# Attention scores as three products of high and low parts, and a bank test for TensorE work, in a two-layer float32 backbone on one core

## The chip, the cores and the metric

The kernel runs on one NeuronCore of a Trainium2 chip. The metric is the device time of one execution in microseconds (us), taken as the median of several runs. Five engines work side by side, each through its own list of instructions in a fixed order: TensorE (PE in the profile, with its weight loads as PEld), VectorE (DVE), ScalarE (ACT), GpSimd (POOL) and SyncE (SP), which issues most of the DMAs. An instruction that waits for another engine holds up everything behind it on its own engine.

## What is computed

Two layers over 256 latent tokens and 256 context tokens of width 2048, batch 1, all inputs float32. Layer 0 projects both streams with one wide matrix, runs 16 heads of neighbourhood attention beside a bidirectional state-space scan, and projects back. Layer 1 is a gated short convolution between two projections. The change touches the attention scores of layer 0 alone:

```python
def na_ssd_mixer(h, hc, w_in, ..., w_out, update_ctx):
    p = h @ w_in
    pc = hc @ w_in[:, base:]
    q = rms_norm(heads(cols(p, COL_Q, NA_WIDTH, 0), NA_HEADS, NA_HEAD_DIM), q_norm_g)
    k = rms_norm(heads(cols(p, COL_K, NA_WIDTH, 0), NA_HEADS, NA_HEAD_DIM), k_norm_g)
    kc = rms_norm(heads(cols(pc, COL_K, NA_WIDTH, base), NA_HEADS, NA_HEAD_DIM), k_norm_g)
    ...
    ya = neighbourhood_attention(q, k, v, kc, vc, rpb).reshape(b, seq, NA_WIDTH)

def row_block(r):    # in neighbourhood_attention, r is a row of the token grid
    s_lat = jnp.einsum('bqhd,bkhd->bhqk', qr, kb).astype(jnp.float32) * scale + bias
    s_lat = jnp.where(mask, s_lat, -jnp.inf)
    s_ctx = jnp.einsum('bqhd,bkhd->bhqk', qr, k_ctx).astype(jnp.float32) * scale
    pr = jax.nn.softmax(jnp.concatenate([s_lat, s_ctx], axis=-1), axis=-1)
    ...
```

A head has 256 queries, 512 keys (256 latent, 256 context) and a head width of 128.

## The kernel before

**Products.** All large projections are made from two parts of each operand: a high part, which is the float32 number rounded to the type float32r, and a low part, which is what the rounding left. A product is then three TensorE products that add up in one bank of PSUM: high by high, high by low, low by high (`mm_act`, L620; `mm_ws`, L630; `mm_both`, L644). The weights come from memory in pieces of 512 KB (`raw`). ScalarE rounds a piece to its high part `wH` (L401), and VectorE subtracts that from the piece to get its low part `wL` (L408). There are three buffers of each, so a piece can be split only when TensorE is done with the piece three before it. The attention proper works in plain float32: the scores (`score`, L998) are one product of `QT` (128 by 128) with `KT` (128 by 512), and each head has two of them, one for each half of its queries. That makes 32 scores in all.

**Stages.** Layer 0 takes the heads in four blocks of four. A block projects Q and K (`do_qk`, L1452; for block 0 the loop at L851), then gate and V, then a quarter of the state-space part (`do_ssd`, L1419). `kq_gen` (L922) turns a block's projected keys or queries into what the scores need: ScalarE sums squares (L928), GpSimd takes the root (L547), VectorE scales (L937), TensorE transposes 128 tokens of four heads into a bank (L950), and that bank is copied to `KT` by ScalarE (L954) or, scaled by the two norm weights `gqk`, to `QT` by VectorE (L956). `head_gen` (L984) then does a head: scores (L1026 to L1032), softmax, transposes of the probabilities, the product with V (L1047), and a write of the gated result to memory. At the end of layer 0 the written results are read back as `mix` (L1478) and projected with `w_out`.

**What sets the order.** The kernel writes its instructions out in Python, and a planner decides where. `Plan` (L38) holds nominal costs and keeps, for each engine, the nominal time at which it is free, and for each buffer the nominal time of its last use (`plan.last`). The main line emits the projections' products. After every few of them `pump` (L269) looks at three lists of tasks (urgent, side, back) and lets a task run on to its next `yield` where `may` (L239) allows it. A `yield W_("PE", tile, nb=1)` asks for TensorE work that reads `tile` and takes one of the eight banks: `may` allows it when a bank is in the free list and the plan has `tile` ready by the plan's TensorE time (L257 to L258). A bank goes into the free list as soon as the instruction that empties it has been emitted, which in the plan may end later than TensorE's present time. When the main line needs banks that are not free, `force` (L290) runs tasks without asking `may`.

Of the kernel before, what the change touches and what calls it, by code (L numbers as in the profile page):

```python
# [8 lines left out]
F32 = mybir.dt.float32  # L9
F32R = mybir.dt.float32r  # L10
AF = mybir.ActivationFunctionType
ALU = mybir.AluOpType
# [129 lines left out]
def kernel(ctx: ExitStack, tc, x, cx, ada_w, ada_b, w_in, w_out, sc_in, sc_out, rpb, small, const,  # L142
                       strict, rows, out):
    nc = tc.nc
# [5 lines left out]
    V, S, G, T, DMA = nc.vector, nc.scalar, nc.gpsimd, nc.tensor, nc.sync  # L150
    DMA2 = nc.scalar
    plan = Plan()
    E = plan.add

    def st(shape, tag, dt=F32, name=None):
        return sb.tile(list(shape), dt, tag=tag, name=name or tag, bufs=1)
# [6 lines left out]
    free_t = [st([128, 512], f"tmp{k}") for k in range(NTMP)]  # L163
# [3 lines left out]
    WH = [st([128, 1024], f"wH{k}", F32R) for k in range(NW)]  # L167
    WL = [st([128, 1024], f"wL{k}", F32R) for k in range(NW)]

    KT, QT, Vt, gt = st([128, 4, 512], "KT"), st([128, 4, 256], "QT"), st([128, 4, 512], "Vt"), st([128, 4, 256], "gt")  # L170
    sz, xtm, yi = st([128, 4, 256], "sz"), st([128, 2, 512], "xtm"), st([128, 4, 256], "yi")
    PT = [st([128, 4, 256], f"PT{k}") for k in range(2)]

# [11 lines left out]
    four = lambda ap: ap.rearrange("p (a b) -> p a b", a=4)  # L185

    def mm(o, l, r, start, stop):
        E(T.matmul(o, l, r, start=start, stop=stop, skip_group_check=True))  # L188
# [12 lines left out]
    def spawn(q, gen, tmps=0, halves=0):  # L201
        q.append(Task(gen, tmps, halves))
# [36 lines left out]
    def may(task, hor, isurg):  # L239
        eng, aps, nb = task.cond  # L240
        if eng == "if":
            return aps()
        if eng == "grow":
            return grow(task)
        if nb and len(free_b) < nb + (0 if isurg else reserve[0]):
            return False
        if eng == "DVE":
            lows_try()
        now, t = plan.t["PE"], plan.t["ACT" if eng == "AQ" else eng]
        rdy = plan.ready(aps)  # L250
        if eng == "AQ":
            return t <= now + hor and rdy <= t
        if hor < 2000 and nb and sorted(plan.last[b.tensor.name] for b in free_b)[nb - 1] + 3000 > now:
            return False
        if hor < 2000:
            rdy += 4000 if eng == "PE" else 0
        if eng == "PE":  # L257
            return rdy + (0 if isurg else 800) <= now + 100  # L258
        if eng == "SP":
            return rdy <= max(t, now) + 200  # L260
        return t <= now + hor and rdy <= max(t, now) + 400
# [68 lines left out]
    def give(pool, *bs):  # L330
        pool.extend(bs)
# [495 lines left out]
    psQ = None  # L827
# [91 lines left out]

    attn = [0]  # L920

    def kq_gen(key, a, ps, nt, stat, dst, banked):  # L922

        for t in range(nt):
            yield W_("ACT", ps[t])
            jk = tmp()
            for h in range(4):
                E(S.activation(jk[:, h * 128:h * 128 + 128], ps[t][:, h * 128:h * 128 + 128], AF.Square,  # L928
                               accum_out=stat[:, 4 * t + h:4 * t + h + 1]))
            give(free_t, jk)  # L930
        yield W_("DVE", stat)
        rstd(stat[:, :4 * nt], stat[:, :4 * nt], 128, EPS, 4 * nt)
        kns = {}

        def norm(t):
            kn = kns[t] = tmp()
            E(V.tensor_tensor(out=four(kn), in0=ps[t].rearrange("p (h d) -> p h d", h=4),  # L937
                              in1=stat[:, 4 * t:4 * t + 4].unsqueeze(2).to_broadcast([128, 4, 128]), op=ALU.mult))
            if banked:
                give(free_b, ps[t])  # L940

        for t in range(nt):
            yield W_("DVE", stat)
            norm(t)
        yield when(lambda: not (attn[0] < 8 * (a if key else 0)))
        for t in range(nt):
            yield W_("PE", kns[t], nb=1)
            pt = bank()
            for h in range(4):
                turn(pt[:, h * 128:(h + 1) * 128], kns[t][:, h * 128:(h + 1) * 128])  # L950
            give(free_t, kns[t])
            yield W_("ACT" if key == "K" else "DVE", pt)
            if key == "K":
                E(S.copy(dst[:, :, t * 128:(t + 1) * 128], four(pt)))  # L954
            else:
                E(V.tensor_scalar(out=dst[:, :, t * 128:(t + 1) * 128], in0=four(pt), scalar1=gqk, scalar2=None, op0=ALU.mult))  # L956
            give(free_b, pt)
        got.add((key, a))

# [24 lines left out]
    def head_gen(a, h):  # L984
        hd = 4 * a + h
        bt, s4, P = bias[hd % 2], s4s[hd % 4], PT[hd % 2]
        yield when(lambda: hd < 2 or ("pv", hd - 2) in got)
        yield W_("SP")
        for r in range(4):
            E(DMA.dma_start(bt[64 * (r % 2):64 * (r % 2) + 64, r // 2, :].rearrange("p (a b) -> p a b", a=4),  # L990
                            bass.AP(tensor=b0.tensor, offset=b0.offset + hd * 64 * 320 + (7 - r) * 31 - 61,
                                    ap=[[319, 64], [31, 4], [1, 64]])))
        yield W_("DVE", bt)
        bv = bt[:, 0:2, :].rearrange("p q (r c) -> p (q r) c", c=64)
        E(V.tensor_tensor(out=bv, in0=bv, in1=mask.unsqueeze(1).to_broadcast([128, 8, 64]), op=ALU.add))
        sps = {}

        def score(qt):  # L998
            ps = bank()
            mm(ps, QT[:, h, qt * 128:(qt + 1) * 128], KT[:, h, :], True, True)  # L1000
            return ps

        def top(qt, ps):
            sp = sps[qt] = tmp()
            E(V.tensor_tensor_reduce(out=two(sp), in0=two(ps), in1=bt[:, 1:3, :] if qt else bt[:, 0::2, :], scale=1.0,
                                     scalar=-3.0e38, op0=ALU.add, op1=ALU.max, accum_out=s4[:, qt:qt + 1]))
            give(free_b, ps)
            E(V.tensor_scalar(out=s4[:, 2 + qt:3 + qt], in0=s4[:, qt:qt + 1], scalar1=-1.0, scalar2=None, op0=ALU.mult))
            yield W_("ACT", sp, s4)
            E(S.activation(sp, sp, AF.Exp, bias=s4[:, 2 + qt:3 + qt], scale=1.0, accum_out=s4[:, 4 + qt:5 + qt]))  # L1010

        def scale_(qt):
            sp = sps[qt]
            E(V.reciprocal(s4[:, 6 + qt:7 + qt], s4[:, 4 + qt:5 + qt]))
            E(V.tensor_scalar(out=sp, in0=sp, scalar1=s4[:, 6 + qt:7 + qt], scalar2=0.5, op0=ALU.mult, op1=ALU.mult))

        def trans(qt):
            pt = bank()
            for kt in range(4):
                turn(pt[:, kt * 128:(kt + 1) * 128], sps[qt][:, kt * 128:(kt + 1) * 128])  # L1020
            give(free_t, sps[qt])
            return pt

        yield when(lambda: ("K", a) in got and ("Q", a) in got)
        yield ("grow", 2, 0)
        yield W_("PE", KT[:, h, :], QT[:, h, :], nb=1)  # L1026
        p0 = score(0)
        yield W_("DVE", p0)
        yield from top(0, p0)
        yield W_("PE", nb=1)  # L1030
        p1 = score(1)
        yield W_("DVE", p1)  # L1032
        yield from top(1, p1)
        yield W_("DVE", sps[0])
        scale_(0)
        yield W_("DVE", sps[1])
        scale_(1)
        for qt in range(2):
            yield W_("PE", sps[qt], nb=1)
            pt = trans(qt)  # L1040
            yield W_("ACT", pt)
            E(S.copy(P[:, :, qt * 128:(qt + 1) * 128], four(pt)))
            give(free_b, pt)
        yield ("cap", 0, 0)
        yield when(lambda: ("V", a) in got and ("G", a) in got)
        yield ("grow", 0, 1)
        yield W_("PE", P, Vt, nb=1)  # L1047
        po = bank()
        for kt in range(4):
            mm(po[:, :256], Vt[:, kt, h * 128:(h + 1) * 128], P[:, kt, :], kt == 0, kt == 3)  # L1050
        got.add(("pv", hd))
        yield W_("DVE", po)
        o = half()
        E(V.tensor_tensor(out=o, in0=po[:, :256], in1=gt[:, h, :], op=ALU.mult))
        give(free_b, po)
        attn[0] += 2
        yield from put_mix(hd, o)
# [350 lines left out]


    Btm[0] = st([128, 2, 4, 128], "Btm", name="Btmt")  # L1410
    spawn(urgent, kq_gen("K", 0, parK, 4, statk, KT, False), 4)
    spawn(urgent, kq_gen("Q", 0, psQ, 2, statq, QT, True), 2)

    def do_g(a, nxt):
        psG = banks(2)
# [36 lines left out]
    def do_qk(a, nxt):  # L1452
        psQ = banks(2)
        proj(512, "act", psQ, 4)
        spawn(urgent, kq_gen("Q", a, psQ, 2, statq, QT, True), 2)
        psK = banks(4)
        proj(512, "act", psK, nxt)
        spawn(urgent, kq_gen("K", a, psK, 4, statk, KT, True), 4)
        for h in range(4):
            spawn(side, head_gen(a, h))  # L1460

# [389 lines left out]
```

## Time and profile before

| | |
|---|---|
| median of 3 runs (lowest to highest) | 1819.94 us (1819.16 to 1823.07) |
| the profiled execution | 1820.47 us |
| span of its instructions | 1818.7 us |
| VectorE busy | 1259.5 us, 69% |
| ScalarE busy | 775.2 us, 43% |
| data moved | 376.90 MB, 207 GB/s over the span |

The rows of a profile are read like this. A group of instructions has its line, engine, operation and tiles (out<-in), the count, the time that they cover, the mean duration of one in ns, and the idle time of the engine ahead of them with what ended it. A timeline row has the start in us, the duration in us, the instruction, and in brackets the idle time of the engine before it. The durations of TensorE products include the time until their results are out, so that products that follow each other overlap in the record: what one costs is the distance from its start to the next one's start. A float32 product stands as two records.

### The profile page before, as it was taken

The page shows a single profiled execution, that of the slowest core. Times are in us where ns is not written, and L with a number is a line of the kernel's source. Part 1 is how long each engine was busy: PE and PEld are TensorE (multiplying, and loading weights), DVE is VectorE, ACT ScalarE, POOL GpSimd, SP SyncE. Part 2 cuts the span into 40 slices and gives each one's busy share as a digit, 9 for nine tenths or more (in the row PEclk, how much of TensorE's full clock was granted, in tenths as well). Part 3 has the DMA queues.
Part 4 walks back from the last instruction along what each step waited for, and adds up shares of the span by engine and source line. Part 5 has one row for each costly group of instructions (what it writes and reads, how often), then busy time and mean ns, then how long its engine had stood idle before and what let it go on. Part 6 is the DMA issues. An engine that isn't in the chain of part 4 may idle for free. (4 is left out here: it accounts for less than half of the span.)

```text
span 1818.7 us, 26323 instructions
## 1 busy us (share of the span) xinstructions
PE 1784.1 (98%) x9961; PEld 1488.1 (82%) x9961; DVE 1259.5 (69%) x2041; ACT 775.2 (43%) x1364; POOL 32.4 (2%) x28
## 2 busy tenths in 40 slices
PE   5999999999999999999999999999999999999998
PEld 4677988878888878888877898788878888888887
DVE  5566775887575877575877686776667776565665
ACT  5422543455232455232454343544445444444442
POOL 0000100001000001000001000000000000000000
PEclk9999999999999999999999999999999999999999
DMA  9987644576655576755576566678867786666664
GB/s 327 339 293 247 214 144 134 171 212 203 216 165 166 169 210 203 218 163 172 167 205 196 163 182 186 195 232 282 270 228 226 232 261 188 187 188 188 187 208 152
DMA packets 249216, 376.90 MB, mean 207 GB/s; under 512 B 32656, under 2 KB 104048, under 8 KB 249088
## 3 DMA queue, kind: packets, MB, share of 16 engines
q1 hardware_dynamic: 239792, 366.64, 65.5%
q10 hardware_dynamic: 9296, 8.57, 1.5%
q8 instruction: 78, 1.28, 0.3%
q14 instruction: 50, 0.41, 0.1%
HBM read 368.70 MB, written 7.77 MB: 207 GB/s over the span
## 5 line engine op out<-in xcount | busy, mean ns | idle before, releaser
L401 ACT CAST wH<-raw 128x1024 fp32r<-128x1024 f32 (+1 forms) x439 | 457.7, 1043 | 710.2 <-PE bank L188 556.2
L408 DVE TENSOR_TENSOR wL<-raw,wH 128x1024 fp32r<-128x1024 f32 (+1 forms) x439 | 532.0, 1214 | 283.8 <-ACT wH L401 281.3
L188 PE MATMUL bank<-h,wH 128*128 128x512 f32 x1024 | 362.4, 399 | 1.5 <-DVE h L1611 0.9
L188 PE MATMUL bank<-hH,wH 128*128 128x256 f32 (+1 forms) x1040 | 353.4, 340 | 0.8 <-ACT wH L401 0.8
L188 PE MATMUL bank<-hL,wH 128*128 128x256 f32 (+1 forms) x1040 | 337.9, 325 | 0.0
L188 PE MATMUL bank<-hH,wL 128*128 128x256 f32 (+1 forms) x1024 | 330.9, 323 | 0.9 <-DVE wL L408 0.9
L188 PE MATMUL bank<-h,wL 128*128 128x256 f32 x1024 | 287.5, 281 | 0.0
L188 PE MATMUL bank<-wH,hH 128*128 128x512 f32 x640 | 258.4, 404 | 3.9 <-ACT hH L738 2.6
L188 PE MATMUL bank<-wL,hH 128*128 128x512 f32 x640 | 251.1, 393 | 0.0
L188 PE MATMUL bank<-wH,hL 128*128 128x512 f32 x640 | 250.3, 392 | 0.1
L188 PEld LDWEIGHTS bank<-h,wH 128*128 128x128 f32 x1024 | 192.4, 188 | 50.5 <-issue 1.6
L795 DVE SCALAR_TENSOR_TENSOR acc<-raw,csil,acc 128x512 f32<-128x512 f32 x256 | 191.9, 749 | 48.5 <-DMA raw<-in_ada_w 37.9
L188 PEld LDWEIGHTS bank<-hH,wH 128*128 128x128 f32 x1040 | 196.5, 189 | 24.1 <-issue 7.2
L188 PEld LDWEIGHTS bank<-hL,wH 128*128 128x128 f32 x1040 | 196.8, 189 | 19.9 <-issue 5.0
L188 PEld LDWEIGHTS bank<-hH,wL 128*128 128x128 f32 x1024 | 193.8, 189 | 18.3 <-DVE wL L408 1.5
L188 PEld LDWEIGHTS bank<-h,wL 128*128 128x128 f32 x1024 | 193.4, 189 | 0.0
L188 PE MATMUL bank<-wH,mix 128*128 128x512 f32 x512 | 163.6, 395 | 0.0
L188 PEld LDWEIGHTS bank<-wH,hH 128*128 128x128 f32 x640 | 120.5, 188 | 35.9 <-issue 7.5
L188 PEld LDWEIGHTS bank<-wH,hL 128*128 128x128 f32 x640 | 120.5, 188 | 26.3 <-DVE hL L744 0.6
L188 PEld LDWEIGHTS bank<-wL,hH 128*128 128x128 f32 x640 | 120.8, 189 | 23.7 <-DVE wL L424 0.3
L188 PEld LDWEIGHTS bank<-wH,mix 128*128 128x128 f32 x512 | 96.1, 188 | 21.3 <-issue 1.5
L188 PE MATMUL bank<-wL,mix 128*128 128x512 f32 x256 | 99.9, 390 | 0.7 <-DVE wL L408 0.7
(246 smaller groups left out, 1665.3 us busy)
## 6 DMA issues: line engine op xcount, KB each, us to landing
raw<-in_w_in SPq DMA_DIRECT2D x208, 512.0 KB, 3.8
raw<-in_ada_w SPq DMA_DIRECT2D x165, 512.0 KB, 4.7
raw<-in_sc_in SPq DMA_DIRECT2D x128, 512.0 KB, 3.8
raw<-in_w_out SPq DMA_DIRECT2D x64, 512.0 KB, 4.8
raw<-in_sc_out SPq DMA_DIRECT2D x32, 512.0 KB, 4.8
tmp<-dram_csr SPq DMA_DIRECT2D x32, 256.0 KB, 5.5
PT<-in_ada_w SPq DMA_DIRECT2D x14, 512.0 KB, 5.8
bias<-dram_rpbs SPq DMA_DIRECT2D x64, 64.0 KB, 3.9
```

What stands on the lines that cost most here:

```text
L188: E(T.matmul(o, l, r, start=start, stop=stop, skip_group_check=True))
L401: E(S.copy(H, v))
L408: E(V.tensor_tensor(out=Lo, in0=v, in1=H.bitcast(F32), op=ALU.subtract))
L795: E(V.scalar_tensor_tensor(out=acc, in0=v[:, j], scalar=csil[:, 2 * k + j:2 * k + j + 1], in1=acc, op0=ALU.mult, op1=ALU.add))
```

## The change

`KT` and `QT` become float32r, and two new tiles `KL` and `QL` hold what the rounding left. In `kq_gen`, ScalarE now writes both high parts from the transposed bank (the copy to `KT` rounds; `QT` is a multiplication by `gqk`, which VectorE did before), and VectorE then subtracts the high part from the same bank to make the low part; the bank is given back only after that. `score` becomes three products into its bank, `QT` by `KT`, `QT` by `KL` and `QL` by `KT`, and waits in the plan for `KL` and `QL`.

The second part is in `may`: where a task asks for TensorE work and for `nb` banks, the plan now also compares with the nominal last use of the bank that it would get. The task runs only when that bank is nominally free, not merely in the free list.

The last line makes room for the 12 KB a partition of the new tiles: the area of SBUF that is kept for the descriptors of one kind of DMA shrinks to 1024 bytes a partition. The program has no such DMA before or after; its DMAs are issued by SyncE and ScalarE.

```diff
@@ -167,7 +167,8 @@
-    KT, QT, Vt, gt = st([128, 4, 512], "KT"), st([128, 4, 256], "QT"), st([128, 4, 512], "Vt"), st([128, 4, 256], "gt")
+    KT, QT, Vt, gt = st([128, 4, 512], "KT", F32R), st([128, 4, 256], "QT", F32R), st([128, 4, 512], "Vt"), st([128, 4, 256], "gt")
+    KL, QL = st([128, 4, 512], "KL", F32R), st([128, 4, 256], "QL", F32R)
@@ -255,6 +256,8 @@
         if eng == "PE":
+            if nb:
+                rdy = max(rdy, sorted(plan.last[b.tensor.name] for b in free_b)[nb - 1])
             return rdy + (0 if isurg else 800) <= now + 100
@@ -948,12 +951,20 @@
             pt = bank()
             for h in range(4):
                 turn(pt[:, h * 128:(h + 1) * 128], kns[t][:, h * 128:(h + 1) * 128])
-            give(free_t, kns[t])
-            yield W_("ACT" if key == "K" else "DVE", pt)
+
+            o = slice(t * 128, (t + 1) * 128)
+            yield W_("ACT", pt)
             if key == "K":
-                E(S.copy(dst[:, :, t * 128:(t + 1) * 128], four(pt)))
+                give(free_t, kns[t])
+                E(S.copy(dst[:, :, o], four(pt)))
+                yield W_("DVE", dst[:, :, o])
+                E(V.tensor_tensor(out=low[:, :, o], in0=four(pt), in1=dst[:, :, o].bitcast(F32), op=ALU.subtract))
             else:
-                E(V.tensor_scalar(out=dst[:, :, t * 128:(t + 1) * 128], in0=four(pt), scalar1=gqk, scalar2=None, op0=ALU.mult))
+                E(S.mul(dst[:, :, o], four(pt), gqk))
+                yield W_("DVE", dst[:, :, o])
+                E(V.scalar_tensor_tensor(out=low[:, :, o], in0=four(pt), scalar=gqk, in1=dst[:, :, o].bitcast(F32),
+                                         op0=ALU.mult, op1=ALU.subtract))
+                give(free_t, kns[t])
             give(free_b, pt)
@@ -997,7 +1008,10 @@
         def score(qt):
             ps = bank()
-            mm(ps, QT[:, h, qt * 128:(qt + 1) * 128], KT[:, h, :], True, True)
+            o = slice(qt * 128, (qt + 1) * 128)
+            mm(ps, QT[:, h, o], KT[:, h, :], True, False)
+            mm(ps, QT[:, h, o], KL[:, h, :], False, False)
+            mm(ps, QL[:, h, o], KT[:, h, :], False, True)
             return ps
@@ -1023,7 +1037,7 @@
-        yield W_("PE", KT[:, h, :], QT[:, h, :], nb=1)
+        yield W_("PE", KL[:, h, :], QL[:, h, :], nb=1)
...
@@ -1837,7 +1851,7 @@
-    nc = bacc.Bacc("TRN2", target_bir_lowering=False, num_devices=1)
+    nc = bacc.Bacc("TRN2", target_bir_lowering=False, num_devices=1, dynamic_dma_scratch_size=1024)
```

The costs in the plan change with this, and so does the order in which the planner writes instructions out. Three places show how. The line numbers of the changed kernel are 3 to 14 higher than before.

The first is TensorE at the first scores of block 0, among the products of the state-space part (`hH`, `hL` are the activations' parts, `wH`, `wL` the weights'). Before:

```order
L188 MATMUL bank_84<-hH_526,wL_102 128x512
L188 MATMUL bank_87<-KT,QT 128x512
L188 MATMUL bank_85<-hH_526,wH_99 128x512
L188 MATMUL bank_85<-hL_531,wH_99 128x512
L188 MATMUL bank_85<-hH_526,wL_102 128x512
```

And now:

```order
L189 MATMUL bank_90<-hH_528,wL_102 128x512
L189 MATMUL bank_85<-KT,QT 128x512
L189 MATMUL bank_85<-KL,QT 128x512
L189 MATMUL bank_85<-KT,QL 128x512
L189 MATMUL bank_87<-hH_528,wH_99 128x512
```

The score stands at the same place, and its one float32 product has become three float32r products into one bank.

The second place is VectorE while block 0 prepares its keys and queries (`tmp_72` is a piece of the state-space convolution, `statq` the queries' norms, `wL_100` the low part of the next weights). Before:

```order
L1167 SCALAR_TENSOR_TENSOR tmp_72<-bank_89,cwh,tmp_72 128x2x254
L1167 SCALAR_TENSOR_TENSOR tmp_72<-bank_89,cwh,tmp_72 128x2x255
L937 TENSOR_TENSOR tmp_65<-bank_87,statq 128x512
L408 TENSOR_TENSOR wL_100<-raw_93,wH_97 128x1024
L937 TENSOR_TENSOR tmp_66<-bank_88,statq 128x512
```

And now:

```order
L1181 SCALAR_TENSOR_TENSOR tmp_72<-bank_89,cwh,tmp_72 128x2x254
L961 TENSOR_TENSOR KL<-bank_90,KT 128x4x128
L1181 SCALAR_TENSOR_TENSOR tmp_72<-bank_89,cwh,tmp_72 128x2x255
L961 TENSOR_TENSOR KL<-bank_91,KT 128x4x128
L940 TENSOR_TENSOR tmp_65<-bank_87,statq 128x512
L411 TENSOR_TENSOR wL_100<-raw_93,wH_97 128x1024
L940 TENSOR_TENSOR tmp_66<-bank_88,statq 128x512
```

Two of the new subtractions now stand ahead of the low part `wL_100`.

The third place is TensorE at the start of the projection with `w_out`, where the last block's V is copied out of its banks (`tmp,xtm` is the state-space part's output, whose bank was one of V's; `mix` are the results read back). Before:

```order
L188 MATMUL bank_85<-wH_97,mix_8754 128x512
L188 MATMUL bank_87<-tmp_68,xtm 64x128
L188 MATMUL bank_87<-tmp_69,xtm 64x128
L188 MATMUL bank_91<-wH_97,mix_8757 128x512
L188 MATMUL bank_91<-wL_100,mix_8757 128x512
```

And now:

```order
L189 MATMUL bank_90<-wH_99,mix_8838 128x512
L189 MATMUL bank_89<-tmp_72,xtm 64x128
L189 MATMUL bank_89<-tmp_67,xtm 64x128
L189 MATMUL bank_86<-wH_97,mix_8835 128x512
L189 MATMUL bank_86<-wL_100,mix_8835 128x512
```

The state-space product stood behind 18 products with `mix`, in the middle of the second piece of weights; now it stands behind 12, between the first piece and the second.

More of the change, by code (lines that the diff above doesn't have):

```diff
@@ L920, with kq_gen @@
     attn = [0]
-    def kq_gen(key, a, ps, nt, stat, dst, banked):
+    def kq_gen(key, a, ps, nt, stat, dst, low, banked):
         for t in range(nt):
@@ L1410 @@
     Btm[0] = st([128, 2, 4, 128], "Btm", name="Btmt")
-    spawn(urgent, kq_gen("K", 0, parK, 4, statk, KT, False), 4)
-    spawn(urgent, kq_gen("Q", 0, psQ, 2, statq, QT, True), 2)
+    spawn(urgent, kq_gen("K", 0, parK, 4, statk, KT, KL, False), 4)
+    spawn(urgent, kq_gen("Q", 0, psQ, 2, statq, QT, QL, True), 2)
     def do_g(a, nxt):
@@ L1454, in do_qk @@
         proj(512, "act", psQ, 4)
-        spawn(urgent, kq_gen("Q", a, psQ, 2, statq, QT, True), 2)
+        spawn(urgent, kq_gen("Q", a, psQ, 2, statq, QT, QL, True), 2)
         psK = banks(4)
         proj(512, "act", psK, nxt)
-        spawn(urgent, kq_gen("K", a, psK, 4, statk, KT, True), 4)
+        spawn(urgent, kq_gen("K", a, psK, 4, statk, KT, KL, True), 4)
         for h in range(4):
```

## The prediction

> **What bounds the kernel now.** I read the page first, then TensorE's waits, then the timeline around one score. The page:
>
> ```profile
> PE 1784.1 (98%) x9961; PEld 1488.1 (82%) x9961; DVE 1259.5 (69%) x2041; ACT 775.2 (43%) x1364; POOL 32.4 (2%) x28
> ...
> PEclk9999999999999999999999999999999999999999
> ```
>
> TensorE is covered for 98% of the span, at full clock in every slice. The ends of its products are modelled, so this alone doesn't show that TensorE is the bound. Its waits and the distance between starts do. TensorE's waits, by what ended them (total us, times, longest):
>
> ```profile
> PE bank L188 <- DVE rx L582: 13.7, 1, 13.7
> PE bank L188 <- ACT hH L738: 2.6, 2, 1.4
> PE bank L188 <- ACT Vt L964: 2.4, 1, 2.4
> PE bank L188 <- DVE half L1374: 1.6, 3, 0.8
> PE bank L188 <- DVE wL L408: 1.6, 3, 0.7
> ```
>
> 13.7 us are the first wait of the program, before any work; the rest are single waits of at most 2.4 us. So wherever the change acts, an instruction less on TensorE should shorten the span by its own length, and an instruction more on another engine costs nothing until TensorE waits for it. One row matters for the second part of the change: the wait of 2.4 us for a copy of V (L964) is a wait for a bank, the only long one.
>
> A score, on TensorE's timeline:
>
> ```profile
> 259.34 0.40 PE L188 MATMUL bank<-hH,wH 128*128 128x512 f32 x1
> 259.57 0.40 PE L188 MATMUL bank<-hL,wH 128*128 128x512 f32 x1
> 259.81 0.40 PE L188 MATMUL bank<-hH,wL 128*128 128x512 f32 x1
> 260.05 1.02 PE L188 MATMUL bank<-KT,QT 128*128 128x512 f32 x2
> 260.50 0.80 PE L188 MATMUL bank<-hH,wH 128*128 128x512 f32 x1
> 261.14 0.39 PE L188 MATMUL bank<-hL,wH 128*128 128x512 f32 x1
> 261.37 0.40 PE L188 MATMUL bank<-hH,wL 128*128 128x512 f32 x1
> ```
>
> The durations (0.40) overlap; the distances between starts are the cost. Three float32r products of 512 columns take 259.34 to 260.05, 0.71 us, or 0.237 each. From the score's start to the second product behind it are 1.09 us (260.05 to 261.14). One float32r product of 0.237 lies in between, whose record starts early at 260.50, so the score itself costs 0.853 us.
>
> **The change, part by part.** *Scores.* One float32 product goes and three float32r products of the same shape come, each with the price of its neighbours above: 0.853 − 0.71 = 0.143 us saved a score. The products at 261.14 and 261.37 start 0.23 apart, so a triple can also cost 0.69; I take 0.15 as between the two. There are 32 scores (64 records at two each, below): 32 × 0.15 = **4.8 us saved**, with 4.6 and 5.3 (0.143 and 0.853 − 3 × 0.23 = 0.163) as ends. The weight loads go from two a score to three:
>
> ```profile
> L188 PEld LDWEIGHTS bank<-KT,QT 128*128 128x128 f32 x64 | 11.5, 189 | 4.8 <-issue 3.1 <-DVE half L1365 0.2
> ```
>
> A load of 189 ns fits under a product of 0.237, so the loads add nothing.
>
> The Trainium skill's page "FP8 and Floating Point Precision", section TensorE Precision Notes, says that a true float32 product is four passes through the array. The two records of 0.853 us agree with that. By the page alone three passes in place of four would save a quarter; what that gives is the fourth rival.
>
> *Keys and queries.* The nearest rows, by shape and source (a bank, 512 columns):
>
> ```profile
> L937 DVE TENSOR_TENSOR tmp<-bank,statk 128x512 f32<-128x512 f32 x12 | 7.6, 684 | 0.8 <-POOL statk L547 0.7
> L956 DVE TENSOR_SCALAR QT<-bank,gqk 128x512 f32<-128x512 f32 x8 | 5.6, 745 | 2.6 <-PE bank L192 2.6
> L975 DVE SCALAR_TENSOR_TENSOR gt<-tmp,bank 128x512 f32<-128x512 f32 x8 | 5.1, 681 | 0.0
> L1161 ACT ACTIVATE tmp<-bank,cbh,cwh 128x512 f32<-128x512 f32 x24 | 18.0, 768 | 0.0
> ```
>
> VectorE gets 16 subtractions for keys at 0.684 and 8 for queries at 0.681, and loses 8 scalings at 0.745: 10.9 + 5.4 − 6.0 = 10.3 us more. ScalarE gets the 8 scalings at about 0.768, 6.1 us; its key copies stay, now with rounding. On TensorE's path all of it counts nothing as long as the weight parts come in time. Their rows:
>
> ```profile
> L408 DVE TENSOR_TENSOR wL<-raw,wH 128x1024 fp32r<-128x1024 f32 x432 | 527.2, 1223 | 283.0 <-ACT wH L401 280.6
> L401 ACT CAST wH<-raw 128x1024 fp32r<-128x1024 f32 x432 | 453.4, 1050 | 693.0 <-PE bank L188 548.8 <-issue 96.0 <-DVE acc L795 12.8
> ```
>
> VectorE waits 281 us for ScalarE's rounding, and ScalarE 549 us for TensorE to let go of a buffer: both run ahead and are held back by TensorE. The tightest place that I found is block 0, where by the order two subtractions now stand ahead of a low part (VectorE, then TensorE's first use):
>
> ```profile
> 222.60 1.22 DVE L408 TENSOR_TENSOR wL<-raw,wH 128x1024 fp32r<-128x1024 f32 x1
> ...
> 226.67 0.28 PE L188 MATMUL bank<-hH,wL 128*128 128x256 f32 x1
> ```
>
> The low part is done at 223.82 and used at 226.67, 2.85 us later. Two subtractions take 1.37 of them; 1.5 remain. I take **0 us**; the ends are 0 and +10.3, if that cover were gone everywhere. The scores must now wait for the subtractions too. In block 0 they come some 30 us later; in block 1 they follow the keys closely (the last two copies of keys, the first score):
>
> ```profile
> 438.20 1.08 ACT L954 COPY KT<-bank 128x512 f32<-128x512 f32 x2 [0.57 <-PE bank L192]
> ...
> 440.58 0.59 PE L188 MATMUL bank<-KT,QT 128*128 128x512 f32 x1
> ```
>
> The copies end at 439.28, and the score starts 1.3 us after. In the changed order 30 products of 256 columns more stand ahead of that score, 3.6 us at 0.12 each (rows under the fifth rival), against four subtractions of 2.7 us. So the planner has paid for them with a later place, and the softmax behind the scores isn't what TensorE waits for.
>
> *The bank test.* It delays work in the program, so it can only help where TensorE sat waiting for a bank. The one place (ACT, PE, DVE rows):
>
> ```profile
> 1162.42 1.07 ACT L1488 CAST mix<-tmp 128x256 fp32r<-128x256 f32 x3 [1.02 <-DMA tmp<-dram_mixd]
> 1164.66 1.55 ACT L964 COPY Vt<-bank 128x512 f32<-128x512 f32 x3
> 1165.28 0.73 PE L188 MATMUL bank<-tmp,xtm 128*64 128x128 f32 x8 [2.42 <-ACT Vt L964]
> 1167.22 1.22 DVE L408 TENSOR_TENSOR wL<-raw,wH 128x1024 fp32r<-128x1024 f32 x1
> 1168.50 0.50 PE L188 MATMUL bank<-wL,mix 128*128 128x512 f32 x1 [0.68 <-DVE wL L408]
> ```
>
> TensorE waits 2.42 us until ScalarE has copied V, and ScalarE was late because it first waited for a DMA that reads `mix` back and then rounded that and a weight. If the product were only put later, TensorE would do `mix` products in the meantime and then stop at 1168.50 all the same: the low part that it needs there is made from 1167.22 on, behind the same ScalarE work, whatever TensorE does. What would be late next is thus that low part, and the gain is 0. In the changed order the whole stretch is dealt out anew: the state-space product stands behind 12 products with `mix` instead of 18, V's copies stand between more roundings of `mix`, and V's product comes earlier too. So the 2.42 + 0.68 us may go, or grow by as much. I take 0, with −3.1 and +3.1 as ends, because the same chain of DMA, rounding and copy stands there in both orders. Beside these TensorE's order changes only by small moves of transposes and the like in layer 0, and not at all after it; the smaller SBUF reserve belongs to a kind of DMA that the program doesn't issue, so 0 for lack of any user.
>
> **Sum.** Against the profiled execution (1820.47 us, of which the span is 1818.7): 1820.5 − 4.8 = 1815.7. It stands 0.5 us above the median of the runs; carried to the median, 1819.9 − 4.8 = **1815.1 us**.
>
> **Rivals.**
> 1. *The bank test pays.* The wait of 2.42 and the next one of 0.68 both go: 1815.1 − 3.1 = 1812.0. For it: that is what the test is made for. Against: the chain above doesn't hang on TensorE, and the test goes by the plan's times, which didn't foresee the DMA; where the plan thinks the bank free, the test does nothing at all.
> 2. *Given back.* The new order puts V's product sooner behind the start of the `mix` products and V's copies behind more roundings; a wait of another 2.4 to 4.8 us there or at a late key bank takes half or all of the gain: 1817.5 to 1819.9, say 1818.7. For it: single waits of 0.7 to 2.4 us do stand in the trace, so the plan errs by that much. Against: the program's other stages pass with almost none.
> 3. *Slower: the subtractions hold up the weights.* VectorE works in order, and each block puts four key subtractions among the low parts of the gate's weights. If these come late, TensorE waits for each: at most 1815.1 + 10.3 = 1825.4. It decides from the point where the 2.85 us at 226.67 are used up, that is with two subtractions more ahead of that low part than the order shows, or with VectorE as much behind. Against: 1.5 us are left there, and VectorE's 281 us of waiting elsewhere.
> 4. *A float32r product costs a quarter of a float32 one.* 0.853 / 4 = 0.213, so 0.213 saved a score, 6.8 in all: 1813.1. Against: the neighbours' 0.23 to 0.237. This is what the Trainium skill's four passes, named above, come to.
> 5. *The loads count.* If TensorE's pace were that of its weight loads, 32 more at 0.189 would add 6.0 us and the products' length would give nothing: 1825.9. Against stand products of 256 columns, each with a load of its own:
>
> ```profile
> 700.10 0.28 PE L188 MATMUL bank<-hL,wH 128*128 128x256 f32 x1
> 700.22 0.28 PE L188 MATMUL bank<-hH,wL 128*128 128x256 f32 x1
> 700.33 0.28 PE L188 MATMUL bank<-hH,wH 128*128 128x256 f32 x1
> ```
>
> They start 0.12 us apart, less than a load's 0.189; loads overlap and don't set the pace. The Trainium skill's "Perfetto Trace Analysis", section Identifying the Most-Contended Engine, would judge TensorE by the busy time of its loads and not of its products: here 82% and not 98%, with the count of loads going up. These rows speak against using it here.
>
> **How the numbers follow.** Forecast 0.54, first rival 0.14, second 0.20, third 0.06, fourth 0.04, fifth 0.02. The forecast's own range is 1813 to 1817.5 (4.6 to 5.3 saved, and small waits that come or go). A measurement of this kernel can tell about 0.2% (3.6 us) from no change, so faster means under 1816.3. Four fifths of the forecast (0.44), the first and the fourth rival give faster: 0.62. The rest of the forecast and most of the second rival give no change: 0.28. The third, the fifth and a tail of the second give slower: 0.10. The range runs from the first rival's 1812 less 1, for a small wait more that goes, to the second's 1819.9: 1811 to 1820.
>
> **What would show it.** The rows of the scores should be 96 of one record, with starts 0.23 to 0.24 us apart and 0.70 to 0.71 a score; 0.64 a score speaks for the fourth rival. TensorE's wait on L408 should stay near 1.6 us; some 10 us more would be the third. Its wait on V's copies and on banks tells the first from the second: gone, or several us in several places. No change in the scores' distance, or VectorE's work on the end of the chain, would make the whole prediction wrong.

## The result and the profile after

The changed kernel takes **1808.6 us** (median of 6 runs, 1807.6 to 1810.3) against 1820.0 for the kernel before (6 runs). The ratio is 0.9937, with a 95% interval of 0.9924 to 0.995: 11.4 us saved, by the interval 9.1 to 13.8. The forecast was 1815.1 with a range of 1811 to 1820, so the kernel gained more than twice the 4.8 us forecast, and lies below the range.

The page of the kernel after, whose profiled execution took 1807.84 us (span 1806.0):

```profile
PE 1777.2 (98%) x9993; PEld 1493.6 (83%) x9993; DVE 1265.9 (70%) x2057; ACT 781.4 (43%) x1372; POOL 31.0 (2%) x28
...
PEclk9999999999999999999999999999999999999999
```

TensorE has 32 records more, as 96 products stand where 64 records stood, and is busy 6.9 us less. VectorE has 6.4 us more work, ScalarE 6.2. The shares look as before: the page alone doesn't tell where 11 us went. TensorE's waits of the kernel after do (in us: total, times, longest):

```profile
PE bank L189 <- DMA raw<-in_ada_w: 14.0, 3, 13.0
PE bank L189 <- ACT hH L741: 2.6, 2, 1.4
...
PE bank L189 <- DVE wL L411: 0.7, 2, 0.4
...
PE bank L189 <- DVE half L1388: 0.2, 1, 0.2
```

The row for V's copies (2.4 us before) is gone; the low parts' fell from 1.6 to 0.7, that of `half` (sums of squares of the state-space groups) from 1.6 to 0.2. No wait after the first 40 us is over 1 us.

A score on TensorE's timeline, after:

```profile
258.86 0.40 PE L189 MATMUL bank<-hH,wL 128*128 128x512 f32 x1
259.09 0.40 PE L189 MATMUL bank<-KT,QT 128*128 128x512 f32 x1
259.33 0.40 PE L189 MATMUL bank<-KL,QT 128*128 128x512 f32 x1
259.56 0.39 PE L189 MATMUL bank<-KT,QL 128*128 128x512 f32 x1
259.79 0.39 PE L189 MATMUL bank<-hH,wH 128*128 128x512 f32 x1
```

From 259.09 to 259.79 are 0.70 us, where a score took 0.853: 0.153 saved, 4.9 for 32. The term of the scores was right.

The mix stage, where the 2.4 us wait had been (PE and ACT rows of the kernel after):

```profile
1151.31 0.39 PE L189 MATMUL bank<-wH,mix 128*128 128x512 f32 x1
...
1152.46 0.58 ACT L975 COPY Vt<-bank 128x512 f32<-128x512 f32 x1
...
1153.77 0.71 ACT L1502 CAST mix<-tmp 128x256 fp32r<-128x256 f32 x2 [0.73 <-DMA tmp<-dram_mixd]
1154.15 0.66 PE L189 MATMUL bank<-tmp,xtm 128*64 128x128 f32 x8
```

V's first copy starts 1.1 us after the first product with `mix` (1151.31); before, the distance was 6.1 us (1158.58 to the 1164.66 that the prediction shows). The state-space product at 1154.15 stands behind 12 such products and waits for nothing.

To see where the time goes by stage, I took the start of the same projection product in two traces and subtracted. Each number of the table is what a kernel's profiled execution gains (+) or loses (−) on that of the kernel before in that stretch of it (us; "layer 1" from 1300 on; e1 to e7 are runs of the next section):

| kernel | 0–205 | block 0, 205–290 | 290–1050 | 1050–1145 | mix stage, 1145–1300 | layer 1 |
|---|---|---|---|---|---|---|
| after | 0.8 | 1.2 | 5.2 | 0.0 | 4.3 | 1.3 |
| e1, products in the old order | −0.2 | −4.3 | 3.0 | −3.6 | 2.8 | 1.3 |
| e2, float32 scores in the new order | 0.2 | 0.3 | 0.5 | −0.2 | 3.5 | 1.3 |
| e3, bank test alone | −0.1 | −0.2 | 0.3 | −4.2 | 1.7 | 0.1 |
| e4, change without the test | 0.0 | −4.8 | 4.9 | 0.0 | 3.5 | 4.0 |
| e5, test in block 0 only | −0.1 | 0.3 | 5.4 | −0.3 | 3.5 | 1.3 |
| e6, test after block 0 only | −0.3 | −5.4 | 5.1 | −0.7 | 4.1 | 5.2 |
| e7, subtractions alone | 0.0 | −4.8 | 0.6 | 0.0 | −0.5 | 0.0 |

Of the 32 scores, six stand in the stretch of block 0, 22 between 290 and 1050 and four in the mix stage, at 0.153 each: 0.9, 3.4 and 0.6 us. So of the 12.7 us by which the two profiled spans differ, the scores have 4.9; some 3.7 are waits and moves of the mix stage, some 1.8 are other waits and small moves between 290 and 1050 (which ones stays open: e2, in the same order, gains only 0.5 there), 1.3 are in layer 1, where TensorE's order is the same, and the rest is the start. The experiments ask which edit brought these.

### The profile page after: what moved, and what is told of

It is laid out like the page before. It is cut to its first block, busy times and chain, and to the rows that moved or that the text cites. A ratio compares the mean times of both kernels' runs of the same rounds, so it can differ in the third digit from the quotient of the medians.

```text
span 1806.0 us, 26436 instructions
## 1 busy us (share of the span) xinstructions
PE 1777.2 (98%) x9993; PEld 1493.6 (83%) x9993; DVE 1265.9 (70%) x2057; ACT 781.4 (43%) x1372; POOL 31.0 (2%) x28
## 5 line engine op out<-in xcount | busy, mean ns | idle before, releaser
L189 PE MATMUL bank<-hH,wH 128*128 128x256 f32 (+1 forms) x1040 | 344.9, 332 | 0.9 <-ACT wH L404 0.9
```

## The experiments

All are timed against the kernel before on the same chip:

| run | median us | lowest to highest | ratio to before, 95% interval |
|---|---|---|---|
| e1_old_order | 1821.06 | 1819.5–1821.5 | 1.0002 (0.9993–1.0011) |
| e2_f32_in_new_order | 1814.55 | 1813.6–1815.4 | 0.9965 (0.9954–0.9977) |
| e3_test_alone | 1821.70 | 1815.6–1823.6 | 1.0005 (0.9993–1.0016) |
| e4_without_test | 1812.99 | 1812.6–1814.6 | 0.9960 (0.9947–0.9973) |
| e5_test_in_block0 | 1808.96 | 1808.2–1810.5 | 0.9939 (0.9926–0.9951) |
| e6_test_after_block0 | 1813.23 | 1810.1–1816.5 | 0.9962 (0.9948–0.9975) |
| e7_subtractions_alone | 1825.23 | 1824.3–1828.0 | 1.0031 (1.0019–1.0042) |
| e8_fourth_product | 1816.55 | 1812.7–1818.2 | 0.9979 (0.9969–0.9988) |
| e9_reads_first | 1820.22 | 1818.2–1823.1 | 1.0000 (0.9991–1.0009) |
| e10_pairs | 1805.03 | 1805.0–1805.6 | 0.9913 (0.9900–0.9927) |
| e11_small_reserve | 1819.31 | 1818.7–1822.8 | 1.0001 (0.9991–1.0010) |
| e12_v_copies_late | 1813.74 | 1810.6–1817.8 | 0.9969 (0.9956–0.9981) |

### Products, order and test apart (e1 to e4)

**e1**: the three products, the subtractions left out of the plan, and the plan told that a score is one float32 product. So the order stays that of before.

```diff
-            mm(ps, QT[:, h, qt * 128:(qt + 1) * 128], KT[:, h, :], True, True)
+            for l, r, first, last in ((QT, KT, True, False), (QT, KL, False, False), (QL, KT, False, True)):
+                T.matmul(ps, l[:, h, o], r[:, h, :], start=first, stop=last, skip_group_check=True)
+            plan.score([QT[:, h, o], KT[:, h, :]], [ps])
```

> The three products a score, with their subtractions, in the order of the kernel before; no bank test. Theory A (products are worth 5 us as forecast, and the other 6.4 us come from the new order): 5 us faster than before, near 1815, with the 2.4 us wait for V's copy and the waits of the softmax factors still there. Theory B (the products themselves are worth the whole 11.4 us, by a shorter product or by what they do to their neighbours): near 1808.6. Theory C (nothing of the gain is the products'): near 1820.

It gave no gain, 1821.1: neither A nor B, and at first sight C. (The expectation's "softmax factors" are the `half` rows.) TensorE's waits in e1:

```profile
PE bank L205 <- DVE wL L425: 3.8, 4, 2.0
...
PE bank L205 <- DVE tmp L1375: 1.5, 1, 1.5
...
PE bank L209 <- DVE KL L972: 0.9, 1, 0.9
```

By the table e1 gains in the two later stages that have scores, while block 0 loses 4.3 in spite of the 0.9 that its scores save, and 3.6 go just ahead of the mix stage. The wait for V's copy that the expectation looked for is down to 0.3: TensorE comes to that stage later. The waits for `wL` and `KL` speak for the forecast's third rival, subtractions that hold up the weights; how they do it is shown at e7.

**e2**: the changed kernel, each score one float32 product, the plan told that it is three.

```diff
-            mm(ps, QT[:, h, o], KT[:, h, :], True, False)
-            mm(ps, QT[:, h, o], KL[:, h, :], False, False)
-            mm(ps, QL[:, h, o], KT[:, h, :], False, True)
+            t1 = T.matmul(ps, QT[:, h, o].bitcast(F32), KT[:, h, :].bitcast(F32), start=True, stop=True, skip_group_check=True)
+            plan.score([QT[:, h, o], KT[:, h, :], KL[:, h, :], QL[:, h, o]], [ps])
```

> The order of the changed kernel on every engine, with one float32 product of the rounded parts in place of three in each score; the low parts of keys and queries are still made but left out of the scores. Theory A: 5 us slower than the changed kernel, near 1813.6, so 6.4 us faster than before by the order alone, with no wait for V's copy. Theory B: near 1820. Theory C: near 1808.6.

1814.55, 5.9 over the changed kernel and 5.5 under the kernel before: theory A in both parts. Half of the gain is the products', half the order's. Of the latter 3.5 us are the mix stage.

**e3**: the kernel before with the test, **e4**: the changed kernel without it. The edit is the same, put in or taken out:

```diff
+            if nb:
+                rdy = max(rdy, sorted(plan.last[b.tensor.name] for b in free_b)[nb - 1])
```

> The kernel before with the bank test alone: the state-space product in the mix stage stands six mix products later, a few transposes move in layer 0. The forecast: 0 us, since the wait for V's copy only turns into one for the low part behind it. The first rival of the forecast (the test pays): 3 to 3.4 us faster than before, near 1816.8, with no TensorE wait over 0.5 us around the V copies. If the whole remainder of 6.4 us were the test's: near 1813.6.

1821.7, no change that can be told: the forecast's 0. Two waits show what happened to the gain (TensorE's timeline in e3):

```profile
1141.21 0.65 PE L188 MATMUL bank<-tmp,xtm 128*64 128x128 f32 x6 [2.06 <-DVE tmp L1353]
...
1170.94 0.50 PE L188 MATMUL bank<-wL,mix 128*128 128x512 f32 x1 [1.53 <-DVE wL L410]
```

The wait for V's copy is gone, and TensorE stands 1.53 us at the low part instead, as the forecast argued, but that is less than the 2.42 and 0.68 of before: by the table the stage gains 1.7. The other wait, at 1141, is another matter: a broadcast read of `dram_csr` came 2.6 us later than in the profile of before (ScalarE waited 3.63 us for it, 1.05 before), and 4.2 us are lost there. e1, in almost the same order, waits there too; e7 below, whose order is that of e1, does not (ScalarE waited 1.66 us). So the order alone doesn't make the read late; what does stays open.

> The changed kernel without the bank test: the state-space product in the mix stage stands six mix products earlier than in the changed kernel. If the test matters: 3 to 6 us slower than the changed kernel, near 1812 to 1815, with a TensorE wait for a bank in the mix stage. If the order that comes with the new scores has by itself put V's copies early enough: within 1 us of the changed kernel, 1808.6, and no such wait.

1813.0, 4.4 over the changed kernel: the test matters, but not where I looked. The mix stage gains 3.5 without it, with a wait of 0.6 for V's copy; the loss is in block 0, 6.0 us against the changed kernel by the table (e4 has 2.7 of them back in layer 1, of which more below). TensorE's waits in e4:

```profile
PE bank L189 <- DVE s L1017: 1.7, 1, 1.7
PE bank L189 <- DVE wL L409: 1.6, 3, 0.7
PE bank L193 <- DVE KL L959: 1.5, 2, 0.9
```

Where the keys are turned in block 0, e4's timeline reads (transposes on PE, the subtraction on DVE):

```profile
220.75 0.68 DVE L959 TENSOR_TENSOR KL<-bank,KT 128x512 fp32r<-128x512 f32 x1
...
221.49 0.66 PE L193 MATMUL bank<-const,tmp 128*128 128x128 f32 x4 [0.91 <-DVE KL L959]
```

and the changed kernel's:

```profile
221.02 0.68 DVE L961 TENSOR_TENSOR KL<-bank,KT 128x512 fp32r<-128x512 f32 x1
...
221.59 0.60 PE L193 MATMUL bank<-const,tmp 128*128 128x128 f32 x4
```

A bank of keys is now held until the subtraction has read it, on top of the copy. Without the test the plan puts the next transpose there as soon as a bank is in the free list, ahead of weight products that could run, and TensorE, which works in order, stands behind it. With the test 18 of those products come first (the transpose stands behind 726 products of the projections and not 708), and it finds its bank free. The waits for `KL` are 1.5 of the 6.0 us. Of the rest, 0.7 are a wait for a low part, 1.7 the wait for `s`, where a state-space product stands behind a score's bank that VectorE reads late, and some 1.7 a fall of the clock behind that wait (last section).

### Where the test pays (e5, e6), and what it pays for (e7)

```diff
-            if nb:
+            if nb and attn[0] < 8:
```

(e6 has `attn[0] >= 8`; `attn` counts the halves of heads that are done, 8 a block.)

> The changed kernel with the bank test only until the heads of attention block 0 are done; its order is that of the changed kernel up to the mix stage, and that of the kernel without the test from there on. Theory D (the test pays by sparing block 0 the waits that the subtractions cause there, 5 to 6 us between 205 and 290 us in the run without the test): as fast as the changed kernel, 1808.6 to 1809.5, the 0.7 us wait for V's copy being all that comes back. Theory E (the test pays in the mix stage): near the run without the test, 1813.

> The mirror image: no bank test until the heads of block 0 are done, then the test; its order is that of the kernel without the test up to the mix stage. Theory D: near the run without the test, 1812 to 1813, with TensorE's waits for KL, wL and s between 205 and 290 us as there. Theory E: near 1808.6.

1809.0 and 1813.2: theory D, in both directions. The test's whole 4.4 us come from block 0, and e6 has its waits for `KL` (1.5 us) and `s` (1.7) as e4 has.

**e7** is e1 with one float32 product of the rounded parts in each score.

> The kernel before, in its order, with the subtractions and the rounded copies added, but each score one float32 product of the rounded parts: the low parts are made and left out of the scores. Theory D: the subtractions cost what the three products gain in the run with the old order, so about 5 us over that run, 1825 to 1827, with the waits for KL and wL in block 0. If the products gained nothing in that run: 1821.

1825.2: 4.2 over e1 and 4.7 over the median of before in that comparison. So the subtractions, in the old order, cost as much as the products gain, and e1's zero was in the main a sum of the two.

Of the 4.8 us that block 0 loses in e7, only 0.95 are a bank held for `KL`. The longest wait is at a low part, behind a DMA. VectorE in the kernel before:

```profile
244.68 0.43 DVE L1087 TENSOR_TENSOR half<-half,half 128x256 f32<-128x256 f32 x1 [3.38 <-DMA half<-in_rows]
```

and SP's queue, VectorE and TensorE in e7:

```profile
243.35 1.58 SPq L1091 DMA_DIRECT2D half<-in_rows  x1
248.45 0.43 DVE L1110 TENSOR_TENSOR half<-half,half 128x256 f32<-128x256 f32 x1 [5.93 <-DMA half<-in_rows]
248.79 3.49 DVE L425 TENSOR_TENSOR wL<-raw,wH 128x1024 fp32r<-128x1024 f32 x3
250.07 0.39 PE L205 MATMUL bank<-hH,wL 128*128 128x256 f32 x1 [1.82 <-DVE wL L425]
```

With the subtractions among VectorE's work, a low part of the weights ends at 236.4 and not 233.1. A load in SP's queue waits for that low part's `raw` buffer, so the read of `in_rows` behind it is issued at 243.35 and not 240.18. VectorE stands for the read, the next low parts come late, and TensorE waits 1.82 us; the clock falls behind that, for some 1.7 more. e1 has the same rows (a wait of 6.09 for the read, then 1.99 at the low part). The changed kernel issues the read at 239.14. So the third rival was real, but by way of a DMA queue: VectorE itself stood idle for 5.93 us ahead of those low parts. The order with the test avoids it.

### The price of a product (e8)

```diff
+            mm(ps, QL[:, h, o], KL[:, h, :], False, True)
```

> The changed kernel with a fourth product in each score, of the two low parts: 32 more products. At 0.23 us each: 7.4 us over the changed kernel, 1816.0, plus or minus 1 for the moves that its plan makes. At a quarter of a float32 product, 0.213: 1815.4. If a product hid behind a neighbour: 1808.6.

1816.55, 7.9 over the changed kernel, 0.248 us for each of 32 more products. With the range of its runs (5.4 us) that bears out 0.23 and can't tell it from 0.213; the timelines above do, with 0.23 to 0.24 between starts.

### The mix stage (e9, e12)

What made V's copies late before? Rows of SP's queue and of ScalarE from the timeline of the kernel before, ahead of the first product with `mix` and at it:

```profile
1132.13 13.33 SPq L371 DMA_DIRECT2D raw<-in_w_out  x4
1145.55 0.93 SPq L1323 DMA_DIRECT2D tmp<-dram_csr  x2
...
1151.92 0.70 ACT L1333 ACTIVATE tmp<-tmp,ncs 128x128 f32<-128x128 f32 x2 [2.99 <-DMA tmp<-dram_csr]
...
1156.77 1.28 ACT L1333 ACTIVATE tmp<-tmp,ncs 128x128 f32<-128x128 f32 x4 [1.51 <-DMA tmp<-dram_csr]
...
1158.58 0.39 PE L188 MATMUL bank<-wH,mix 128*128 128x512 f32 x1
```

The reads of `dram_csr` stand behind four weight loads, which hold SP's queue for 13 us as each waits for a buffer, and ScalarE then waits for the reads, 2.99 and 1.51 us. In the changed order they stand two loads earlier. **e9** moves only that, in the kernel before, by holding back two loads of `w_out`:

```diff
+            if nwo[0] in (2, 3) and ncsr[0] < 13 + nwo[0] and loads and loads[0][2] is w_out:
+                return
```

> The kernel before with one thing moved in SP's queue: the last two pairs of broadcast reads of dram_csr (the cumulative sums of the last state-space block) stand behind two and three loads of w_out, as in the changed kernel, and no longer behind four and five. Everything ahead of the mix stage stays as before; the plan deals out the mix stage itself anew. Theory F (V's copies were late because ScalarE waited for these reads, and the new order put the reads earlier): TensorE's waits of 2.4 us for V's copy and 0.7 us for the low part go, 3 to 4 us faster than before, near 1816.5. Theory G (the reads have nothing to do with it; the gain of the mix stage comes from elsewhere in the new order): 1820, with the wait for V's copy there.

1820.2: theory F falls as it was put. Two rows of e9:

```profile
1160.93 1.06 ACT L968 COPY Vt<-bank 128x512 f32<-128x512 f32 x2
...
1161.56 0.40 PE L188 MATMUL bank<-tmp,xtm 128*64 128x128 f32 x2 [1.73 <-ACT Vt L968]
```

V's copies came 2.8 us earlier in the stage (3.3 us after its first product, not 6.1), but the plan put the product that needs the bank earlier too, behind 9 products with `mix` instead of 18. The wait is a difference: the end of V's first copy less the product's place at 0.235 us a product. Counted from the first product with `mix`:

| kernel | V's first copy ends | products ahead | difference | wait seen |
|---|---|---|---|---|
| before | 6.7 | 18 (4.2) | 2.5 | 2.4 |
| e9 | 3.9 | 9 (2.1) | 1.8 | 1.7 |
| e4 | 2.1 | 6 (1.4) | 0.7 | 0.6 |
| e1 | 4.5 | 18 (4.2) | 0.3 | 0.3 |
| e3 | 5.0 | 24 (5.6) | −0.7 | none |
| after | 1.7 | 12 (2.8) | −1.1 | none |

**e12** delays V's first copy in the changed kernel, and with it what ScalarE does behind it; the order stays:

```diff
+            if a == 3 and t == 0:
+                for _ in range(9):
+                    S.copy(Vt[:, t, :], ps[t])
             E(S.copy(Vt[:, t, :], ps[t]))
```

> The changed kernel, in its own order, with nine more ScalarE copies of the same part of V (unplanned, about 5 us) ahead of V's first copy in the mix stage, so that V's copies end as late behind the first product with mix as in the kernel before (6.1 us in place of 1.1 at the start of the first). Theory H (the mix stage gains by V's copies being in time): TensorE stands 3 to 4.5 us at the state-space product, where the traces so far give a wait of the first copy's end less the product's place (6.7 less 11 products of 0.235), and perhaps 1 us at a low part; 1812 to 1814. Theory I (their time doesn't matter there): 1808.6 to 1809.

1813.7, 5.1 us slower, theory H. V's first copy ends at 8.0, which less 2.8 for the 12 products is 5.2; the wait, 5.15, is longer than the 3 to 4.5 expected because the copy was later than the 6.7 aimed at. ScalarE and TensorE in e12:

```profile
1159.04 0.59 ACT L978 COPY Vt<-bank 128x512 f32<-128x512 f32 x1
...
1159.68 0.69 PE L189 MATMUL bank<-tmp,xtm 128*64 128x128 f32 x3 [5.15 <-ACT Vt L978]
```

So shown: V's copies in time, together with the product's later place, are the gain of the mix stage, and the whole order brings that (e2). Not settled: which pieces of the order bring V's copies forward; the reads alone (e9) brought them 2.8 us of the 5.0.

### Layer 1, and the reserve (e10, e11)

The changed kernel gains 1.3 us in layer 1, where both kernels issue the same products. There products of 512 and 256 columns alternate (TensorE's timeline, after):

```profile
1600.04 0.28 PE L189 MATMUL bank<-h,wL 128*128 128x256 f32 x1
1600.16 0.40 PE L189 MATMUL bank<-h,wH 128*128 128x512 f32 x1
...
1601.10 0.28 PE L189 MATMUL bank<-h,wL 128*128 128x256 f32 x1
```

Six products take 1.06 us here. In e4 the same stretch has 1.04, and in the changed kernel the stretch from 1426 to 1491. A stretch keeps its pace until some transposes come in between (at 1425 and 1491), and behind them has one of the two. **e10** issues the products in twos:

```diff
-            mm(o, H[:, bb], act, first, False)
-            mm(o[:, :256], Lo[:, bb], act[:, :256], False, last)
+            for c in (b, b + 1):
+                mm(ps[c], H[:, c * 128:(c + 1) * 128], act, first, False)
+            for c in (b, b + 1):
+                mm(ps[c][:, :256], Lo[:, c * 128:(c + 1) * 128], act[:, :256], False, last)
```

> The changed kernel with the products of the last layer's first projections in another order: for each two banks both products with the high part of the weights (512 columns), then both with the low part (256), where they alternated. In the traces six products of this stage start in 1.06 us or in 1.04 us, for whole stretches, at a granted clock of 1.00. If alternating is what lengthens them: 339 times 0.02, up to 5.5 us faster than the changed kernel, near 1803. If not: 1808.6, or a random share of it.

1805.0, the fastest of all, 3.6 us under the changed kernel's median (the two ratios' intervals just touch, 0.9927 and 0.9924). Eight products of e10:

```profile
1599.61 0.63 PE L189 MATMUL bank<-h,wH 128*128 128x512 f32 x2
1600.08 0.39 PE L189 MATMUL bank<-h,wL 128*128 128x256 f32 x2
1600.31 0.62 PE L189 MATMUL bank<-h,wH 128*128 128x512 f32 x2
1600.77 0.40 PE L189 MATMUL bank<-h,wL 128*128 128x256 f32 x2
1601.00 0.63 PE L189 MATMUL bank<-h,wH 128*128 128x512 f32 x2
```

They take 1.39 us, which is 1.04 for six, all through the layer. So the 1.3 us belong to a pace that the change did not set on purpose: that part of the gain is luck.

**e11** is the smaller reserve alone:

```diff
-    nc = bacc.Bacc("TRN2", target_bir_lowering=False, num_devices=1)
+    nc = bacc.Bacc("TRN2", target_bir_lowering=False, num_devices=1, dynamic_dma_scratch_size=1024)
```

> The kernel before with the smaller SBUF reserve alone, in an identical order. The forecast counts it at 0: 1820. If the places of the tiles in SBUF decide how fast the products start (6 in 1.04 or 1.06 us in the last layer): up to 1.3 us faster in that stage, 1818.7.

1819.3, a ratio of 1.0001: no change that can be told, as forecast. Its profile gains 1.1 us in layer 1, but the reserve can't be what sets the pace there: by the same subtraction e9 gains 1.3 with the old reserve, and e7 none with the new one.

## Why the prediction was wrong

- *Scores, −4.8*: right. 0.153 us a score on the timeline; e2 puts the products at 5.9 us and e7 against e1 at 4.2, on either side of it.
- *Keys and queries, 0*: right for the changed kernel, for a reason that the step didn't have. It weighed one tight place, 2.85 us ahead of a low part against 1.37 of subtractions. But a subtraction also holds a bank, and what stands behind that on TensorE are transposes (0.9 to 1.5 us in e1, e4 and e7); and it delays low parts that a load in SP's queue waits for, and so a read behind that load (1.8 us at the low part in e7). Without the bank test the subtractions cost some 5 to 6 us in block 0 (e7 by itself; e1 and e4 with the 0.9 that the scores save there). VectorE's work grew by 6.4 us of busy time and not by the 10.3 of the sum.
- *Bank test, 0 with ends of 3.1*: **the step that failed**, in both of its arguments. It looked for the test's worth at "the one place" where the kernel before waited for a bank. Alone, on that kernel, the test indeed measures as 0 (e3). (Its profile gains 1.7 in the mix stage and loses 4.2 ahead of it at a late read.) In the changed kernel it is worth 4.4 us (e4), all in block 0 (e5, e6), where the kernel before had no such wait, since the change's own subtractions make it.
- "*The same chain of DMA, rounding and copy stands there in both orders*", and TensorE's order changes "only by small moves": the failed reason for taking the new order at 0. The order alone brings 5.5 us (e2), 3.5 of it in the mix stage (and 1.3 the pace in layer 1, where TensorE's order is the same: luck), where V's first copy went from 6.1 to 1.1 us behind the first product. The chain is the same, its place in time is not, and the forecast had named the new place of V's copies without pricing it. That end of the range was −3.1, near enough for the mix stage, but it was given to the test's rival with 0.14 instead of to the order.
- *Reserve, 0*: right (e11).
- The rivals: the first had the mix stage's size (3.1 against 3.5 in e2) with the wrong cause, so by luck. The second didn't come. The third existed and was cancelled by another part of the change. The fourth is excluded by the starts, 0.23 apart and 0.70 a score, not 0.64. The fifth is excluded by e8, whose 32 more products and loads cost a product's time each, and by the scores, which got faster with 32 more loads.

By terms: 4.9 from the products, 5.5 from the order with the test in it, and the rest, 1.0, within the spread of the runs.

## What to carry to other kernels

Price a guard not only against the waits of the kernel that you have, but against those that the other edits of the same change would make without it: the test was worth 0 alone and 4.4 us beside the subtractions. Where a planner deals out a stage anew, the wait at a place is a difference of two times, the producer's end and the consumer's place. Read both off the new order with the old durations before taking the term at 0. And an operation added to an engine that has time to spare can cost elsewhere: here by how long it kept a bank taken, and by a DMA that came late because a load ahead of it in the queue waited for a buffer.

## What the runs showed of the hardware

**Short waits often halved TensorE's clock.** After a wait on TensorE the granted clock often fell to 0.50 for 3.4 us. Products of 512 columns then started 0.43 us apart instead of 0.23 (e4, 272.60 to 274.74), so that about half of the 3.4, 1.7 us, was lost on top of the wait (an estimate). In e4, behind the 1.7 us wait at 271.0, three stretches read (start and end, length, busy us and instructions of PE, PEld, DVE, ACT and POOL, granted clock, DMA share, GB/s):

```profile
268.00:271.50 3.50, 1.80 (x10) 1.24 (x9) 3.39 (x9) 0.73 (x2) 0.00 (x0) 1.00 0.06 6
271.80:275.20 3.40, 3.40 (x11) 2.72 (x11) 1.84 (x7) 0.20 (x2) 0.00 (x0) 0.50 0.43 148
275.20:279.00 3.80, 3.80 (x27) 3.39 (x26) 1.45 (x6) 1.03 (x5) 0.00 (x0) 1.00 0.00 0
```

In the 14 profiles there are 13 waits of 1.53 to 5.15 us between 100 us and the end. Ten were followed by such a fall; those of 1.53 (e3), 1.61 (e6) and, though longer, 2.42 us (the profile of before) were not. No wait under 1.5 us there was. In the first 100 us, left out here, six of the profiles have a fall too, at 27.5 to 29.0 us, about 1 us behind a wait of only 1.2 us that follows other short ones. The Trainium skill, on the page "TensorE: Matmul & The Clock Gate", section "Why this matters for your kernels", advises against gaps of more than about 3 us between bursts of products. Here 1.55 us was enough (e1, the wait that ends at 1142.05). The changed kernel has no such wait after its start, and no fall there.

**A pace that locks in.** Alternating float32r products of 512 and 256 columns ran at 1.06 or 1.04 us for six, at a granted clock of 1.00, for up to 220 us at a time; the pace changed only where other work came in between. Issued in twos they kept 1.04. Why is open.
